# Low parts of the weights: an accumulating transfer onto a negated high part, in place of a VectorE subtraction

## The chip, the core and the metric

The kernel runs on one core of one Trainium2 chip. The metric is the device time of one execution in microseconds, the median of several runs. The kernel before takes 2429.83 us (three runs, 2429.18 to 2433.76). The engines are named as the profile names them: PE (TensorE, with PEld for its weight loads), DVE (VectorE), ACT (ScalarE), POOL (GpSimd), SP (SyncE, which here only issues transfers).

## What is computed

Two blocks of a language model in float32, one behind the other, on 512 tokens of width 1024. The first block has two layers: a hybrid mixer (gated linear attention beside stick-breaking attention) and a convolution mixer, each followed by a SwiGLU of width 2816. The second block has differential attention and a short convolution, each followed by a squared-ReLU MLP of width 4096. Cut to what matters here, everything the change touches is a product of activations with a weight:

```python
def swiglu(h, wg, wu, wd):
    return (jax.nn.silu(h @ wg) * (h @ wu)) @ wd

def sq_relu_mlp(x, w_up, w_down):
    return jnp.square(jax.nn.relu(x @ w_up)) @ w_down
```

## The kernel before

PE multiplies in a format (float32r) that keeps fewer bits than float32. The kernel therefore splits each operand into a high part (the value rounded to float32r) and a low part (the value minus the high part), and forms each product as three matmuls, in `mm3`: high weight by high input, high weight by low input, low weight by high input (L297, L298, L299).

A weight arrives by SP's queue in a buffer `wraw` of 128 x 2048 elements (1 MB; three such buffers), from `load_w` (L286) or `load_blocks` (L477, L480). `w_parts` turns half a buffer at a time, called a part here (128 x 1024 elements, 512 KB), into a tile `wh` and a tile `wl`, of which there are four each:

```python
act.activation(v(wh), src, AF.Copy)
dve.tensor_sub(v(wl), src, v(b(wh)))
```

ACT's line reads as L102 in the profile, since all ACT instructions go through one wrapper; DVE's is L273. There are 488 parts in the program.

Two kinds of stage use them. In most stages (`group` and its relatives: projections, and `out_proj`) a part meets all 512 tokens: eight blocks of 128 x 128, three matmuls each. In the up projections, `group_s` multiplies 2 x 2 blocks of weights and inputs in seven products instead of eight. It loads two `wraw` buffers, with the blocks b11, b12 in the first and b21, b22 in the second, and needs seven parts: b11, b22 and b21 as they are loaded, and four that DVE forms in place in `wraw`. A product is 8 blocks x 3 matmuls of 256 columns. There are 34 calls, in 14 runs of calls between two `out_proj`: 3, 4 and 3 in each SwiGLU (L856), and 1, 2, 2 and 2 in each MLP (L1398); the first group of each of the four layers is a plain one. The order of the code in a call is:

```python
o11 = parts(b11)
dve.tensor_sub(b11, b12, b11)           # L524
product(g, parts(b11), sums(0), True)
o22 = parts(b22)
dve.tensor_sub(b12, b22, b12)           # L533
dve.tensor_sub(b22, b11, b22)           # L534
product(a, parts(b22), sums(1))
```

Then follow the product with `o22`, those of b12 and b21, `dve.tensor_add(b21, b21, b22)` (L547), and the product of the new b21. Since L524, L534 and L547 overwrite a block that has just been split, each must wait until everything that reads the old block is done. ACT also copies three of the products out of PSUM (p1, p5, u2), and applies the activation function and the split of the results, in `evac`.

A scheduler gives every engine one fixed order of instructions from the program text; each engine then takes its list in that order, waiting at whatever is not ready. POOL's list before holds 173 rows: small set-up work and elementwise sums such as L862 (`pool_e.tensor_add` in SwiGLU's `down_evac`) and L406, L1092 (sums of squares).

Of the kernel before, what the change touches and what calls it, by code (L numbers as in the profile page):

```python
# [12 lines left out]
AF = mybir.ActivationFunctionType  # L13
# [96 lines left out]
def body(ctx: ExitStack, tc: tile.TileContext, A, out, consts):  # L110
    nc = tc.nc
    real_act, dve, pool_e, pe, sync = nc.scalar, nc.vector, nc.gpsimd, nc.tensor, nc.sync

    act = Act(tc, real_act)
# [70 lines left out]
    b = lambda t: t.bitcast(F32)  # L185
# [81 lines left out]
    def w_parts(src, n):  # L267
        n_p[0] += 1
        wh = wpool.tile([P, 1024], F32R, tag="wh", name=f"wh{n_p[0]}", bufs=4)
        wl = wpool.tile([P, 1024], F32R, tag="wl", name=f"wl{n_p[0]}", bufs=4)  # L270
        v = (lambda t: t[:, :n]) if len(src.shape) == 2 else (lambda t: t[:, :n].rearrange("p (k c) -> p k c", k=src.shape[1]))
        act.activation(v(wh), src, AF.Copy)
        dve.tensor_sub(v(wl), src, v(b(wh)))  # L273
        return wh, wl

    def load_w(parts, k0, nk):

        n_w[0] += 1
        i = n_w[0]
        cols = sum(c1 - c0 for _, c0, c1 in parts)  # L280
        n = nk * cols
        raw = wpool.tile([P, 2048], F32, tag="wraw", name=f"wraw{i}", bufs=3)
        rv = raw[:, :n].rearrange("p (k c) -> p k c", k=nk)
        o = 0
        for ap, c0, c1 in parts:
            sync.dma_start(rv[:, :, o : o + c1 - c0], ap[k0 * P : (k0 + nk) * P, c0:c1].rearrange("(k p) c -> p k c", p=P))  # L286
            o += c1 - c0
        assert nk % 2 == 0
        hi, lo = [], []
        for h in range(2):  # L290
            wh, wl = w_parts(raw[:, h * n // 2 : (h + 1) * n // 2], n // 2)
            for t, ks in ((wh, hi), (wl, lo)):
                ks += [t[:, k * cols : (k + 1) * cols] for k in range(nk // 2)]
        return hi, lo
# [189 lines left out]
    def group_plain(w0, w1, evac, at):  # L484


        ws = []
        for rv in load_blocks(w0, w1):
            for h in range(2):
                wh, wl = w_parts(rv[:, 2 * h : 2 * h + 2, :].rearrange("p k c -> p (k c)"), 1024)  # L490
                ws += [(wh[:, k * T : (k + 1) * T], wl[:, k * T : (k + 1) * T]) for k in range(2)]
        for th, tr in enumerate((T0, T1)):
            pss = [bank(), bank()]
            for k in range(8):
                for n in range(2):
                    for p in range(2):
                        wh, wl = (t[:, n * 256 + p * P : n * 256 + (p + 1) * P] for t in ws[k])
                        mm3(pss[n][:, p * 256 : (p + 1) * 256], wh, wl, xh[k][:, tr], xl[k][:, tr], k == 0 and p == 0, k == 7)
                if (th, k) in at:
                    at[th, k]()  # L500
            for n in (1, 0):
                evac(n, th, pss[n], False)

    def group_s(w0, w1, evac):
# [13 lines left out]
        xs = lambda k0, tr: lambda k: (xh[k0 + k][:, tr], xl[k0 + k][:, tr])  # L518
        sums = lambda n: lambda k: (so[0][:, k, n, :], so[1][:, k, n, :])
        parts = lambda t: w_parts(t, 1024)  # L520

        a, d, g = bank(), bank("at"), bank("at")
# [981 lines left out]
```

## Time and profile before

| | |
|---|---|
| Median of 3 runs | 2429.83 us |
| The profiled execution's own time | 2430.2 us |
| Its span, first to last instruction | 2428.4 us |
| PE, PEld busy | 2374.3, 2056.2 us |
| DVE busy, instructions | 1576.9 us, 2105 |
| ACT busy, instructions | 1185.1 us, 2005 |
| POOL busy, instructions | 218.8 us, 193 |
| SP's transfers | 204.72 MB, 26.0% of 16 engines' span |
| Mean granted TensorE clock | 0.988 |

Shares are of the span. PE's busy time counts overlapping matmuls and says little of its rate; how far apart matmuls start, in the rows in order of time, says more. A DMA share is the busy share of the core's 16 DMA engines. The granted clock is a share of 2.4 GHz, so 0.50 is 1.2 GHz.

### The profile page before, as it was taken

How to read it: one execution, taken by the hardware profiler on the slowest of the kernel's cores; microseconds unless marked ns; L12 is line 12 of the kernel's file. 1: busy time of each engine (PE TensorE's matmuls, PEld its weight loads, DVE VectorE, ACT ScalarE, POOL GpSimd, SP SyncE). 2: the span in 40 equal slices, each digit the busy share in tenths (PEclk: the TensorE clock that was granted, in tenths of full speed). 3: DMA queues.
4: the chain of work that ended last, by engine and by line, in shares of the span. 5: the costliest groups of instructions: out<-in, count | busy, mean ns of one | idle time of the engine just before them, and what ended most of it. 6: DMA issues, size and time to landing. Idle time of an engine off the chain costs nothing. (4 is left out here: it accounts for less than half of the span.)

```text
span 2428.4 us, 34281 instructions
## 1 busy us (share of the span) xinstructions
PE 2374.3 (98%) x14106; PEld 2056.2 (85%) x14106; DVE 1576.9 (65%) x2105; ACT 1185.1 (49%) x2005; POOL 218.8 (9%) x193
## 2 busy tenths in 40 slices
PE   8999999999999899999999999899999999899998
PEld 6667798989887799898987778898998888888998
DVE  4333685868799978585755775754577644854664
ACT  4663553434664655252444555653554224653553
POOL 0000000111002210202000003100003102100001
PEclk9999999999999899999999999999999999999999
DMA  5112223232312023232332112222332232223331
GB/s 166 36 52 70 70 84 108 88 122 70 122 53 69 18 70 122 87 105 91 111 108 66 53 53 70 87 71 95 130 101 74 87 104 78 79 71 104 122 99 41
DMA packets 148109, 206.91 MB, mean 85 GB/s; under 512 B 5822, under 2 KB 88305, under 8 KB 147953
## 3 DMA queue, kind: packets, MB, share of 16 engines
q1 hardware_dynamic: 147921, 204.72, 26.0%
q8 instruction: 110, 1.80, 0.3%
q14 instruction: 46, 0.38, 0.0%
q10 hardware_dynamic: 32, 0.01, 0.0%
HBM read 202.61 MB, written 2.10 MB: 84 GB/s over the span
## 5 line engine op out<-in xcount | busy, mean ns | idle before, releaser
L297 PE MATMUL ps<-rs,wh 128*128 128x256 f32 (+1 forms) x3216 | 1084.9, 338 | 9.4 <-ACT rs L102 4.1
L299 PE MATMUL ps<-rs,wl 128*128 128x256 f32 (+1 forms) x3216 | 1081.3, 337 | 10.3 <-DVE wl L273 10.3
L298 PE MATMUL ps<-rs,wh 128*128 128x256 f32 (+1 forms) x3216 | 1080.8, 336 | 0.0
L273 DVE TENSOR_TENSOR wl<-wraw,wh 128x1024 fp32r<-128x1024 f32 (+1 forms) x488 | 597.2, 1232 | 482.0 <-ACT wh L102 480.4
L102 ACT ACTIVATE wh<-wraw 128x1024 fp32r<-128x1024 f32 (+1 forms) x488 | 508.3, 1047 | 673.3 <-PE ps L298 546.1
L297 PEld LDWEIGHTS ps<-rs,wh 128*128 128x128 f32 x3216 | 611.1, 190 | 78.3 <-ACT rs L102 4.8
L299 PEld LDWEIGHTS ps<-rs,wl 128*128 128x128 f32 x3216 | 611.1, 190 | 77.7 <-DVE wl L273 12.1
L298 PEld LDWEIGHTS ps<-rs,wh 128*128 128x128 f32 x3216 | 610.8, 190 | 67.7 <-issue 2.9
L102 ACT ACTIVATE fs<-fs 128x512 f32<-128x512 f32 (+2 forms) x365 | 205.2, 571 | 93.6 <-DVE fs L1154 20.2
L299 PE MATMUL ps<-ph_so,wl 128*128 128x256 f32 x816 | 233.9, 287 | 4.1 <-DVE wl L273 3.9
L297 PE MATMUL ps<-ph_so,wh 128*128 128x256 f32 x816 | 232.6, 285 | 3.7 <-ACT wh L102 3.5
L298 PE MATMUL ps<-ph_so,wh 128*128 128x256 f32 x816 | 231.7, 284 | 0.0
L102 ACT ACTIVATE fs<-ps 128x512 f32<-128x512 f32 (+1 forms) x202 | 112.6, 562 | 138.0 <-PE ps L299 106.1
L299 PEld LDWEIGHTS ps<-ph_so,wl 128*128 128x128 f32 x816 | 157.5, 193 | 7.5 <-DVE wl L273 7.5
L297 PEld LDWEIGHTS ps<-ph_so,wh 128*128 128x128 f32 x816 | 157.5, 193 | 4.9 <-ACT wh L102 4.4
L298 PEld LDWEIGHTS ps<-ph_so,wh 128*128 128x128 f32 x816 | 157.5, 193 | 0.0
L102 ACT ACTIVATE rs<-fs 128x512 fp32r<-128x512 f32 (+1 forms) x153 | 91.9, 607 | 84.9 <-DVE fs L846 45.3
L429 DVE TENSOR_TENSOR rs<-fs,rs 128x512 fp32r<-128x512 f32 (+1 forms) x132 | 86.6, 663 | 18.3 <-ACT rs L102 17.9
L862 POOL TENSOR_TENSOR fs<-fs,fs 128x512 f32<-128x512 f32 x32 | 52.3, 1634 | 474.3 <-DVE fs L860 474.3
L102 ACT ACTIVATE rs<-fs,vec 128x256 fp32r<-128x256 f32 (+1 forms) x104 | 58.4, 585 | 62.0 <-POOL fs L1122 19.0
L406 POOL TENSOR_TENSOR fs<-fs,fs 128x512 f32<-128x512 f32 x28 | 46.3, 1653 | 385.7 <-ACT fs L102 373.7
L955 PE MATMUL ps<-rs,rs 128*128 128x256 f32 (+20 forms) x339 | 71.3, 364 | 1.1 <-DVE rs L1045 0.6
(303 smaller groups left out, 2160.9 us busy)
## 6 DMA issues: line engine op xcount, KB each, us to landing
wraw<-in_mlp_w_up_dram SPq DMA_DIRECT2D x32, 1024.0 KB
wraw<-in_mlp_w_down_dram SPq DMA_DIRECT2D x32, 1024.0 KB
wraw<-in_ffn_w_up_dram SPq DMA_DIRECT2D x44, 512.0 KB
wraw<-in_ffn_w_gate_dram SPq DMA_DIRECT2D x44, 512.0 KB
wraw<-in_ffn_w_down_dram SPq DMA_DIRECT2D x20, 1024.0 KB
wraw<-in_cv_w_pw_dram SPq DMA_DIRECT2D x16, 512.0 KB
wraw<-in_attn_w_qkv_dram SPq DMA_DIRECT2D x16, 512.0 KB
wraw<-in_conv_w_in_dram SPq DMA_DIRECT2D x16, 512.0 KB
```

Source lines behind the costliest of these rows:

```text
L102: r = self.engine.activation(out, in_, func, **kw)
L273: dve.tensor_sub(v(wl), src, v(b(wh)))
L297: pe.matmul(ps, wh, h, start=start, stop=False, skip_group_check=True)
L298: pe.matmul(ps, wh, l, start=False, stop=False, skip_group_check=True)
L299: pe.matmul(ps, wl, h, start=False, stop=stop, skip_group_check=True)
L406: r = eng.tensor_add(acc, acc, s)
L429: dve.tensor_sub(l, src, b(h))
L862: pool_e.tensor_add(res[o], res[o], s)
L955: pe.matmul(pc[:, y - t0 : t1 - t0], d, x[:, y - s : t1 - s], start=i == 0, stop=i == len(todo) - 1, skip_group_check=True)
```

## The change

`w_parts` alone changes. ACT writes the high part twice: once into `wh`, and once, times -1, into `wl`. The low part then comes about in `wl` by a transfer that GpSimd issues: it reads the raw weight and adds it to what `wl` holds, so that `wl` becomes weight minus high part. DVE's subtraction is gone. The lines below it in the file move down by one (L524 becomes L525 and so on).

```diff
--- before.py
+++ after.py
@@ -270,7 +270,8 @@
         wl = wpool.tile([P, 1024], F32R, tag="wl", name=f"wl{n_p[0]}", bufs=4)
         v = (lambda t: t[:, :n]) if len(src.shape) == 2 else (lambda t: t[:, :n].rearrange("p (k c) -> p k c", k=src.shape[1]))
         act.activation(v(wh), src, AF.Copy)
-        dve.tensor_sub(v(wl), src, v(b(wh)))
+        act.activation(v(wl), src, AF.Copy, scale=-1.0)
+        nc.gpsimd.dma_start(out=v(wl), in_=src, accum_op=mybir.AluOpType.add)
         return wh, wl
 
     def load_w(parts, k0, nk):
```

Every part therefore loses one DVE instruction, gains one ACT instruction and one transfer of 512 KB within SBUF. 488 transfers join POOL's list, which grows from 173 rows to 661; DVE's shrinks from 2104 to 1616 and ACT's grows from 1808 to 2321.

On ACT, in one call of `group_s` in the first SwiGLU (the call with part numbers 82 to 88 and the buffers wraw34, wraw35; `fs` are scratch tiles, `ps` PSUM banks, `rs` split activations; what a row waits for stands in brackets), the order before was:

```order
L102 ACTIVATE wh82_3734<-wraw34_3725 128x1024 [waits DMAHW7_49,PE_49]
L102 ACTIVATE fs17_98<-fs17_98 128x512 [waits DVE_49]
L102 ACTIVATE wh83_3764<-wraw34_3725 128x1024 [waits DVE_49,PE_49,Activation_49]
L102 ACTIVATE wh84_3793<-wraw35_3728 128x1024 [waits DMAHW2_49,PE_49,Activation_49]
L102 ACTIVATE fs23_104<-fs23_104 128x512 [waits DVE_49]
L102 ACTIVATE rs11_76<-fs17_98 128x2x256 [waits DVE_49]
L102 ACTIVATE rs11_76<-fs23_104 128x2x256 [waits DVE_49]
L102 ACTIVATE fs26_107<-ps139_3731 128x512 [waits PE_49]
L102 ACTIVATE wh85_3799<-wraw35_3728 128x1024 [waits DVE_49,Activation_49]
L102 ACTIVATE wh86_3855<-wraw34_3725 128x1024 [waits Activation_49]
L102 ACTIVATE wh87_3886<-wraw35_3728 128x1024 [waits DMAHW1_49,PE_49,Activation_49]
```

and is now, up to the fourth part:

```order
L102 ACTIVATE wh82_3815<-wraw34_3806 128x1024 [waits DMAHW7_49,Activation_49]
L102 ACTIVATE fs23_104<-fs23_104 128x512 [waits DVE_49]
L102 ACTIVATE wl82_3816<-wraw34_3806 128x1024 [waits DMASW5_49]
L102 ACTIVATE rs11_76<-fs17_98 128x2x256 [waits DVE_49]
L102 ACTIVATE wh83_3846<-wraw34_3806 128x1024 [waits DVE_49,PE_49,Activation_49]
L102 ACTIVATE rs11_76<-fs23_104 128x2x256 [waits DVE_49]
L102 ACTIVATE wl83_3847<-wraw34_3806 128x1024 [waits DMASW6_49,PE_49]
L102 ACTIVATE fs26_107<-ps139_3812 128x512 [waits PE_49]
L102 ACTIVATE wh84_3876<-wraw35_3809 128x1024 [waits DMAHW2_49,Activation_49]
L102 ACTIVATE wl84_3877<-wraw35_3809 128x1024 [waits DMASW7_49]
L102 ACTIVATE wh85_3883<-wraw35_3809 128x1024 [waits DVE_49]
```

Each `wh` is followed by a `wl`, with work on the results of the call before in between. `wh83`, the split of the new b11, still stands behind DVE's subtraction, and so does `wh85`.

On DVE, at the same place, from the first part's low part to the second's, before:

```order
L273 TENSOR_TENSOR wl82_3735<-wraw34_3725,wh82_3734 128x1024 [waits DMAHW7_49,Activation_49]
L524 TENSOR_TENSOR wraw34_3725<-wraw34_3725 128x4x256 [waits DMAHW0_49,DVE_49]
L542 TENSOR_TENSOR fs23_104<-ps136_3506,fs23_104 128x512 [waits PE_49]
L533 TENSOR_TENSOR wraw34_3725<-wraw35_3728,wraw34_3725 128x4x256 [waits DMAHW2_49,DVE_49]
L843 TENSOR_TENSOR fs23_104<-fs23_104,fs11_92 128x512 [waits DVE_49]
L545 TENSOR_TENSOR fs16_97<-ps137_3507,fs16_97 128x512 [waits PE_49]
L273 TENSOR_TENSOR wl83_3765<-wraw34_3725,wh83_3764 128x1024 [waits Activation_49]
```

and now, from the first subtraction in place to the last:

```order
L525 TENSOR_TENSOR wraw34_3806<-wraw34_3806 128x4x256 [waits DMAHW0_49,DMAHW7_49,DMASW6_49,DMASW1_49]
L847 TENSOR_TENSOR fs23_104<-ps136_3580,fs23_104 128x512 [waits PE_49]
L534 TENSOR_TENSOR wraw34_3806<-wraw35_3809,wraw34_3806 128x4x256 [waits DMAHW2_49,DVE_49]
L430 TENSOR_TENSOR rs13_78<-fs23_104,rs11_76 128x2x256 [waits Activation_49]
L535 TENSOR_TENSOR wraw35_3809<-wraw34_3806,wraw35_3809 128x4x256 [waits DMASW3_49,DMASW6_49,DVE_49,Activation_49]
L540 TENSOR_TENSOR fs24_105<-ps141_3814,fs24_105 128x512 [waits Activation_49]
L548 TENSOR_TENSOR wraw35_3809<-wraw35_3809 128x4x256 [waits DMAHW1_49,DMASW6_49,DVE_49]
```

The low parts (L273) are gone from the list, and the in-place operations on b11, b22 and b21 (L525, L535, L548) now wait for a transfer of GpSimd's queue (DMASW): that of part 82, 84 and 87, which read the old block.

On POOL, at the end of `out_proj` in the first SwiGLU, where L863 (L862 before) stood alone, now:

```order
L274 DMA wl102_4469<-wraw41_4466 128x1024 [waits DMAHW2_49,DMASW1_49,Activation_49]
L863 TENSOR_TENSOR fs3_84<-fs3_84,fs13_94 128x512 [waits DVE_49]
L274 DMA wl103_4474<-wraw41_4466 128x1024 [waits DMASW2_49,Activation_49]
L274 DMA wl104_4544<-wraw42_4534 128x4x256 [waits DMAHW3_49,DMASW3_49,Activation_49]
L863 TENSOR_TENSOR fs4_85<-fs4_85,fs9_90 128x512 [waits DVE_49]
L863 TENSOR_TENSOR fs5_86<-fs5_86,fs19_100 128x512 [waits DVE_49]
L274 DMA wl105_4575<-wraw42_4534 128x4x256 [waits DMASW4_49,Activation_49]
```

The transfers stand between POOL's sums in one list.

## Rows read from the trace of the kernel before

**Rows 1.** Page, part 1: busy time, share of the span, instructions of each engine.

```profile
PE 2374.3 (98%) x14106; PEld 2056.2 (85%) x14106; DVE 1576.9 (65%) x2105; ACT 1185.1 (49%) x2005; POOL 218.8 (9%) x193
```

**Rows 2.** Page, part 4: the chain that ended last, by engine.

```profile
PE 34%; DVE 4%; ACT 1%; issue 0%; POOL 0%; DVEq 0%; POOLq 0%
```

**Rows 3.** Waits of PE: line, releaser, total us, times, longest.

```profile
PE ps L299 <- DVE wl L273: 14.2, 11, 2.7
```

**Rows 4.** Page, part 5: groups by line; busy us, mean ns, idle before.

```profile
L273 DVE TENSOR_TENSOR wl<-wraw,wh 128x1024 fp32r<-128x1024 f32 (+1 forms) x488 | 597.2, 1232 | 482.0 <-ACT wh L102 480.4
L102 ACT ACTIVATE wh<-wraw 128x1024 fp32r<-128x1024 f32 (+1 forms) x488 | 508.3, 1047 | 673.3 <-PE ps L298 546.1
L862 POOL TENSOR_TENSOR fs<-fs,fs 128x512 f32<-128x512 f32 x32 | 52.3, 1634 | 474.3 <-DVE fs L860 474.3
```

**Rows 5.** ACT in order of time, 446 to 470 us: start, us, instruction, idle before.

```profile
446.67 0.64 ACT L102 ACTIVATE fs<-fs 128x512 f32<-128x512 f32 x1 [0.58 <-DVE fs L843]
449.15 1.06 ACT L102 ACTIVATE wh<-wraw 128x1024 fp32r<-128x1024 f32 x1 [1.84 <-DVE wraw L524]
...
453.74 0.64 ACT L102 ACTIVATE rs<-fs 128x512 fp32r<-128x512 f32 x1 [1.37 <-DVE fs L846]
...
456.61 0.58 ACT L102 ACTIVATE fs<-ps 128x512 f32<-128x512 f32 x1
...
462.58 0.60 ACT L102 ACTIVATE fs<-ps 128x512 f32<-128x512 f32 x1 [1.70 <-PE ps L299]
...
469.39 1.06 ACT L102 ACTIVATE wh<-wraw 128x1024 fp32r<-128x1024 f32 x1 [1.84 <-DVE wraw L524]
```

**Rows 6.** DVE in order of time, 445 to 470 us: start, us, instruction.

```profile
445.23 0.68 DVE L539 TENSOR_TENSOR fs<-ps,fs 128x512 f32<-128x512 f32 x1
...
446.56 1.22 DVE L273 TENSOR_TENSOR wl<-wraw,wh 128x1024 fp32r<-128x1024 f32 x1
447.81 1.23 DVE L524 TENSOR_TENSOR wraw<-wraw 128x1024 f32<-128x1024 f32 x1
...
468.05 1.22 DVE L524 TENSOR_TENSOR wraw<-wraw 128x1024 f32<-128x1024 f32 x1
```

**Rows 7.** PE in order of time, a 256-column stretch and a 512-column one.

```profile
447.33 0.28 PE L299 MATMUL ps<-rs,wl 128*128 128x256 f32 x1
447.45 0.28 PE L297 MATMUL ps<-rs,wh 128*128 128x256 f32 x1
...
18.71 0.40 PE L374 MATMUL ps<-wl,rs 128*128 128x512 f32 x1
18.95 0.40 PE L375 MATMUL ps<-wh,rs 128*128 128x512 f32 x1
```

**Rows 8.** Windows: length, busy us (x) by engine, PEclk, DMA share, GB/s.

```profile
core 0: us, PE busy (x) PEld busy (x) DVE busy (x) ACT busy (x) POOL busy (x), PEclk, DMA share, GB/s
447.80:468.00 20.20, 20.16 (x170) 19.96 (x169) 18.36 (x20) 11.30 (x14) 0.00 (x0) 1.00 0.35 108
439.50:444.00 4.50, 4.50 (x40) 4.50 (x40) 2.96 (x3) 2.97 (x4) 0.00 (x0) 1.00 0.60 191
820.00:840.00 20.00, 10.53 (x33) 8.04 (x34) 18.92 (x49) 11.02 (x29) 1.32 (x1) 0.62 0.04 12
1531.00:1552.00 21.00, 16.84 (x106) 15.83 (x107) 19.53 (x19) 14.19 (x23) 7.91 (x4) 0.84 0.12 41
```

**Rows 9.** Page, part 3: the queue that carries the weights: packets, MB, share.

```profile
q1 hardware_dynamic: 147921, 204.72, 26.0%
```

**Rows 10.** SP's issue of the first load, and PE's first matmul on it.

```profile
0.74 0.38 SPq L202 DMA_DIRECT2D ident<-consts_dram  x1
...
2.82 0.28 PE L255 MATMUL ps<-ident,ph_stage 16*128 16x16 f32 x1 [2.82 <-DMA ident<-consts_dram]
```


## The prediction

> **What bounds the kernel now.** I read the page's busy times first, then the chain, then what PE waits for. PE is busy for 98% of the span [rows 1], and the chain that ended last runs through PE for most of its named part [rows 2]. PE waits for a low part on 11 occasions, 14.2 us in all [rows 3]. So the work that the change takes away from DVE, 488 subtractions of 1232 ns, 597.2 us [rows 4], lies beside PE's; at most those 14.2 us and a little of the time at the ends of stages are to be won. What may be lost is larger, and the question is whether the new way of making a low part still keeps ahead of PE.
>
> How far ahead it must be is read from the rows in order of time. In a call of group_s, matmuls of 256 columns start 0.12 us apart (447.33, 447.45), so a product of 24 takes 24 x 0.118 = 2.83 us, and a new part is due every 2.83 us. The window shows the 0.118: 20.20 us for 170 matmuls, 7 x 24 = 168 of them [rows 7, 8]. In the other stages matmuls of 512 columns start 0.24 us apart [rows 7], and a part lasts 5.7 us. Two starts of L524 in calls that follow each other are 468.05 - 447.81 = 20.24 us apart: that is the period of a call, and PE is busy for 20.16 of 20.20 us in it [rows 6, 8].
>
> **Removed.** 597.2 us of DVE, beside PE: at most about 14 us on the path [rows 3, 4]. I take 0, since the wait that stood there comes back as a longer one.
>
> **Added on ACT.** 488 more writes of the kind that takes 1047 ns [rows 4], 511 us; ACT goes from 1185 to 1696 us of 2428, busy but no bound by sum.
>
> **Added on the DMA engines.** No row shows a transfer within SBUF or one that adds. The nearest rows are the weight loads: 191 GB/s at a share of 0.60, so 318 GB/s at full share [rows 8]. A part of 524,288 bytes takes 1.65 us at that rate if an adding transfer moves like a load; 3.3 us if reading both operands halves the rate; 6.6 us at a quarter. I take 3.3, because the destination has to be read as well as the source, and keep 1.65 and 6.6 as ends. In total 488 x 3.3 = 1610 us, plus 26.0% of 2428 = 631 us for the loads [rows 9]: 2241 us, below the span.
>
> The Trainium skill, in Collectives: The Full Stack, section The bandwidth ceiling, says the same of reductions in the DMA path: 32 against 62 GB/s, because the add needs two source reads. By it the term is the 3.3 us; no run here shows it yet.
>
> **The time to landing, L.** The first load's issue ends at 0.74 + 0.38 = 1.12 us, and PE starts on it at 2.82 [rows 10]: 1.7 us, of which 64 KB take 0.2, so 1.5 us are fixed. L is 1.5 + 1.65 = 3.2 us at the least and 1.5 + 6.6/0.83 = 9.5 at the most; I take 1.5 + 3.3/0.83 = 5.5, where 0.83 is what a call's loads leave free (0.35 of 20.2 us [rows 8] is 7 us, 17% of the 40 us that I find below). GpSimd's own time to issue a transfer is in no row; it is one reason to keep the upper end.
>
> The Trainium skill, in DMA: Bandwidth & Descriptors, section Anatomy of one DMA, fits GpSimd's transfers by 2.0 us plus bytes at 436 GB/s. By that estimate L is 3.2 us, and the sum would be that of the first rival.
>
> **One call of group_s.** Three operations in place on DVE (the new b11, b22, b21) now wait for a landed transfer, and behind each stands an ACT write, with everything else in ACT's list behind that. I walk round a call by durations of [rows 5, 6]: ACT write 1.06, DVE operation 1.23, ACT copy out of PSUM 0.58, activation or split 0.63, DVE sum 0.68.
> - From the issue of b11's transfer: L, L525 1.23, then on ACT wh 1.06, split 0.63, wl 1.06, copy of p1 0.58, b22's wh and wl 2.12. Together L + 6.7, and b22's transfer is issued.
> - From there: L, L535 1.23, wh 1.06, copy of p5 0.58, wl 1.06. Together L + 3.9, and the transfer of the new b22 is issued.
> - From there: L, then two products 5.66 and a sum 0.68 that stand ahead of L548 on DVE (b21's transfer, third in its queue, lands at about the same time, L + 6.6); L548 1.23; wh, activation and wl 2.74; the next call's wh, activation and wl 2.74. Together L + 13.0, and the next call's b11 is issued.
>
> Round the call: 3L + 23.6 = 40.1 us, against 20.24 now: 19.9 us more. Of the 34 calls, 20 follow another call and pay in full: 20 x 19.9 = 398 us. The first call of each of the 14 runs is prepared in part beneath the end of out_proj; four tiles of wl let that be two or three parts, so I charge half: 14 x 9.9 = 139 us.
>
> **The other parts**, 488 - 34 x 7 = 250, cost 0: the DMA engines need 3.3 + 1.65 us for one and for its load, PE takes 5.7, and four tiles allow 3 x 5.7 = 17 us of lead against 2 x 1.06 + 5.5. If that cover goes (a transfer of 6.6 us, 8.3 with its load), each costs 2.6 us, 650 in all.
>
> **Ends of stages.** Where PE already waits for a low part [rows 3] the subtraction of 1.23 us becomes 1.06 + 5.5: 11 x 5.3 = 58 us. POOL's sums, 1.6 us each [rows 4], and the transfers now wait for each other in one list. I cost that at 0, since the lead of 17 us hides it outside group_s; without it each of the 32 L863 delays a part by its 1.6 us, 52 us in all.
>
> **The clock.** In the span's worst gap, PE busy for 10.53 of 20 us, the granted clock was 0.62; at 16.84 of 21 it was 0.84 [rows 8]. In a call of 40 us PE would be busy for half. At 1.2 GHz the two products on the path take 5.66 us more, 34 x 5.66 = 192 us; I take half, 96, as the clock is low for part of the time.
>
> **Sum.** 2430 + 398 + 139 + 58 + 96 = 3121 us, made against the profiled execution (2430.2 us; the median is 2429.83, so no correction). I predict 3120 us. The measurement tells changes of about 0.2% (5 us) from none.
>
> **Rivals.**
> 1. *The transfers are cheap.* L = 3.2 and 1.65 us each. Round the call 3 x 3.2 + 23.6 = 33.2, 13 more: 20 x 13 + 14 x 6.5 = 351; ends 11 x 3.0 = 33; clock 0. 2815 us. For it: the engines are idle for two thirds of the time. Against it: it lets the second read cost nothing. Chance 0.17.
> 2. *The transfers become the bound*, by DMA engines at a quarter of a load's rate or by GpSimd's issue taking as long. 488 x 6.6 + 631 = 3850 us, with gaps some 3950. For it: nothing in the trace shows such a transfer's price. Against it: nothing shows one so slow. Chance 0.23.
> 3. *Faster.* DVE's freed time reaches PE's waits: the 14.2 us of [rows 3] go, 2416 us. It decides at the point where a second write and a landing take no longer than the subtraction: 1.06 + L below 1.23. The least fixed time, 1.5 us, is above that already. Chance 0.02.
> 4. *No effect.* The scheduler's lead hides all of it in group_s too. That needs a round of at most 20.24 us, which is less than its 23.6 without any L. Chance 0.01: 2430 us.
>
> **Numbers.** The forecast keeps 0.57. It is slower by over 0.2% in three cases, 0.57 + 0.17 + 0.23 = 0.97; faster 0.02; within 0.2% 0.01. The range reaches below the first rival (2815), as the part of a round that is hidden may be larger than I charge, and up to the second's: 2700 to 3950. It leaves out some 0.15: still slower transfers, and the two cases without a loss.
>
> **What would show it.** In the profile after: DVE's 488 subtractions gone, ACT's writes at about 976 and 1020 us, a GpSimd queue with 488 transfers and about 256 MB. Starts of L525 in calls that follow each other should be 36 to 45 us apart, with ACT idle before wh until DVE's L525, L535 and L548, and DVE idle until a transfer. Out_proj and the projections should stay near their old pace. I am wrong in the main step if the period of a call is below 30 us; wrong in the price of a transfer if the projections are stretched too, or if the transfers' share of the engines is far from 1610 us.

## The result, and the profile after

The changed kernel takes 3129.91 us (median of 4 runs, 3123.56 to 3132.5), 1.287 times the kernel before, 95% interval 1.2849 to 1.289. The forecast was 3120 us. The loss is 700 us.

The page of the profile after, line by line: busy times, the DMA queues, the chain that ended last, two groups of instructions, and the transfers with their size and median time to landing:

```profile
PE 2607.1 (84%) x14106; PEld 2223.7 (71%) x14106; DVE 1018.3 (33%) x1617; ACT 1610.7 (52%) x2493; POOL 710.0 (23%) x681
...
q0 software_dynamic: 161664, 252.80, 46.9%
q1 hardware_dynamic: 147921, 204.72, 20.2%
...
PE 12%; DMA 8%; issue 5%; ACT 4%; DVE 2%; POOL 1%; POOLq 0%; DVEq 0%; ACTq 0%
...
L274 POOL DMA_DIRECT2D wl<-wraw x488 | 523.7, 1074 | 2097.8 <-ACT wl L102 1885.5
...
L102 ACT ACTIVATE wl<-wraw 128x1024 fp32r<-128x1024 f32 (+1 forms) x488 | 504.8, 1034 | 15.3 <-PE ps L375 15.3
...
wl<-wraw POOLq DMA_DIRECT2D x476, 512.0 KB, 5.2
```

DVE is down to 1018.3 us from 1576.9 [rows 1], and it helped nothing: PE's share fell from 98% to 84%. ACT has its 488 second writes, 504.8 us (2493 instructions against 2005 [rows 1]). A queue that was not there before carries 252.80 MB at 46.9% of 16 engines, beside the loads' 20.2%; the loads themselves moved the same 204.72 MB as in [rows 9]. From the start of its issue on GpSimd a transfer takes 5.2 us to land. The chain could be followed back only to 2145 us, so its shares, 32% in all, speak of the last third of the span; the transfer has 8%.

Who waited for whom (engine, line, releaser: us in total, times, longest):

```profile
engine line waited for: us in total, times, longest us
PEld ps L300 <- DMA wl<-wraw: 408.2, 152, 6.4
...
DVE wraw L535 <- DMA wl<-wraw: 240.8, 33, 10.2
...
ACT wh L102 <- DVE wraw L535: 201.4, 32, 7.1
DVE wraw L525 <- DMA wl<-wraw: 196.7, 33, 37.6
...
ACT wh L102 <- DVE wraw L525: 159.5, 25, 11.4
...
ACT wh L102 <- DVE wraw L548: 70.2, 32, 3.5
...
DVE wraw L548 <- DMA wl<-wraw: 32.4, 20, 3.3
```

PE's weight loads wait 408 us for a landed low part, where before they waited 19.6 us for DVE's low part (PE's matmuls then: 14.2 us [rows 3]). The lines of DVE and ACT in pairs are the mechanism: DVE's L535 waits for a transfer, 240.8 us, and ACT's next split waits for L535, 201.4; the same for L525, 196.7 and 159.5. L548 waits for a transfer only 32.4 us in all, because L540 ahead of it on DVE has waited already; what releases it is read from one call below.

One call of group_s in order of time, the counterpart of [rows 5, 6]. ACT (start, us, instruction, idle before and what ended it):

```profile
543.25 1.06 ACT L102 ACTIVATE wh<-wraw 128x1024 fp32r<-128x1024 f32 x1 [5.78 <-DVE wraw L525]
...
546.16 1.04 ACT L102 ACTIVATE wh<-wraw 128x1024 fp32r<-128x1024 f32 x1
547.11 1.04 ACT L102 ACTIVATE wl<-wraw 128x1024 fp32r<-128x1024 f32 x1
555.27 1.06 ACT L102 ACTIVATE wh<-wraw 128x1024 fp32r<-128x1024 f32 x1 [7.12 <-DVE wraw L535]
...
556.71 1.05 ACT L102 ACTIVATE wl<-wraw 128x1024 fp32r<-128x1024 f32 x1
...
568.24 0.60 ACT L102 ACTIVATE fs<-ps 128x512 f32<-128x512 f32 x1 [6.70 <-PE ps L300]
571.13 1.06 ACT L102 ACTIVATE wh<-wraw 128x1024 fp32r<-128x1024 f32 x1 [2.29 <-DVE wraw L548]
```

DVE in the same call:

```profile
541.91 1.23 DVE L525 TENSOR_TENSOR wraw<-wraw 128x1024 f32<-128x1024 f32 x1 [3.72 <-DMA wl<-wraw]
...
554.01 1.23 DVE L535 TENSOR_TENSOR wraw<-wraw,wraw 128x1024 f32<-128x1024 f32 x1 [8.45 <-DMA wl<-wraw]
568.87 0.69 DVE L540 TENSOR_TENSOR fs<-ps,fs 128x512 f32<-128x512 f32 x1 [13.64 <-ACT fs L102]
569.81 1.22 DVE L548 TENSOR_TENSOR wraw<-wraw 128x1024 f32<-128x1024 f32 x1 [0.25 <-DMA wl<-wraw]
...
582.36 1.23 DVE L525 TENSOR_TENSOR wraw<-wraw 128x1024 f32<-128x1024 f32 x1 [3.24 <-DMA wl<-wraw]
```

POOL, the issue of the transfers of b22, of the new b22, of b21 and of the next call's b11:

```profile
548.44 1.28 POOL L274 DMA_DIRECT2D wl<-wraw  x1 [1.09 <-ACT wl L102]
558.05 1.28 POOL L274 DMA_DIRECT2D wl<-wraw  x1 [8.33 <-ACT wl L102]
...
561.84 1.28 POOL L274 DMA_DIRECT2D wl<-wraw  x1 [0.61 <-ACT wl L102]
...
576.96 1.30 POOL L274 DMA_DIRECT2D wl<-wraw  x1 [1.52 <-DVE fs L546]
```

ACT writes b22's negated high part from 547.11 on, for 1.04 us. GpSimd issues the transfer at 548.44. DVE's L535, which overwrites b22, starts at 554.01, after 8.45 us of waiting; ACT's next write starts when L535 has ended, at 555.27, after 7.12 us. Then ACT waits 6.70 us for the product that needs the new b22 (568.24), and L540 and L548 follow. L548 has one more wait: it starts at 569.81, 0.25 us after L540 has ended, when b21's transfer, issued at 561.84, has landed. By the issue and the landing of each transfer in the trace, L548 starts within 0.3 us of b21's landing in 29 of the 34 calls; so b21's is the third landing of the round, more often than the new b22's. From one L525 (541.91) to the next (582.36) it takes 40.45 us, against 20.24 before [rows 6].

Windows of the profile after: two calls in the first SwiGLU, one in the second, and the entry to an out_proj:

```profile
core 0: us, PE busy (x) PEld busy (x) DVE busy (x) ACT busy (x) POOL busy (x), PEclk, DMA share, GB/s
541.90:582.40 40.50, 28.07 (x164) 26.56 (x164) 10.89 (x14) 17.45 (x21) 8.97 (x7) 0.75 0.73 141
582.40:621.60 39.20, 26.33 (x168) 24.89 (x168) 10.81 (x13) 17.45 (x21) 8.96 (x7) 0.80 0.75 145
1113.80:1153.30 39.50, 25.50 (x169) 24.18 (x168) 11.65 (x15) 17.86 (x22) 8.95 (x7) 0.86 0.69 126
660.00:680.00 20.00, 15.48 (x66) 12.34 (x66) 1.39 (x2) 6.43 (x7) 2.57 (x3) 0.91 0.94 243
```

In a call PE is busy for 25 to 28 of 40 us at a clock of 0.75 to 0.86; before it was 20.16 of 20.20 at 1.00 [rows 8].

### The profile page after: what moved, and what is told of

Its sections match the earlier page's. It is cut to its first block, busy times and chain, and to the rows that moved or that the text cites. A ratio compares the mean times of both kernels' runs of the same rounds, so it can differ in the third digit from the quotient of the medians.

```text
span 3121.4 us, 35667 instructions
## 1 busy us (share of the span) xinstructions
PE 2607.1 (84%) x14106; PEld 2223.7 (71%) x14106; DVE 1018.3 (33%) x1617; ACT 1610.7 (52%) x2493; POOL 710.0 (23%) x681
## 3 DMA queue, kind: packets, MB, share of 16 engines
q0 software_dynamic: 161664, 252.80, 46.9%
q1 hardware_dynamic: 147921, 204.72, 20.2%
## 5 line engine op out<-in xcount | busy, mean ns | idle before, releaser
L298 PE MATMUL ps<-rs,wh 128*128 128x256 f32 (+1 forms) x3216 | 1124.8, 350 | 72.3 <-ACT wh L102 41.8
L299 PE MATMUL ps<-rs,wh 128*128 128x256 f32 (+1 forms) x3216 | 1111.3, 346 | 0.0
L274 POOL DMA_DIRECT2D wl<-wraw x488 | 523.7, 1074 | 2097.8 <-ACT wl L102 1885.5
L298 PEld LDWEIGHTS ps<-rs,wh 128*128 128x128 f32 x3216 | 645.2, 201 | 156.5 <-ACT wh L102 51.9
L299 PEld LDWEIGHTS ps<-rs,wh 128*128 128x128 f32 x3216 | 644.6, 200 | 67.3 <-issue 2.1
L102 ACT ACTIVATE wl<-wraw 128x1024 fp32r<-128x1024 f32 (+1 forms) x488 | 504.8, 1034 | 15.3 <-PE ps L375 15.3
L300 PE MATMUL ps<-ph_so,wl 128*128 128x256 f32 x816 | 282.6, 346 | 199.4 <-DMA wl<-wraw 199.3
L300 PEld LDWEIGHTS ps<-ph_so,wl 128*128 128x128 f32 x816 | 200.5, 246 | 214.6 <-DMA wl<-wraw 214.6
L298 PE MATMUL ps<-ph_so,wh 128*128 128x256 f32 x816 | 279.0, 342 | 45.1 <-ACT wh L102 41.6
L299 PE MATMUL ps<-ph_so,wh 128*128 128x256 f32 x816 | 270.6, 332 | 0.0
L298 PEld LDWEIGHTS ps<-ph_so,wh 128*128 128x128 f32 x816 | 199.1, 244 | 59.6 <-ACT wh L102 50.1
L299 PEld LDWEIGHTS ps<-ph_so,wh 128*128 128x128 f32 x816 | 198.3, 243 | 0.0
L540 DVE TENSOR_TENSOR fs<-ps,fs 128x512 f32<-128x512 f32 x34 | 23.5, 692 | 407.6 <-ACT fs L102 407.6
L535 DVE TENSOR_TENSOR wraw<-wraw,wraw 128x1024 f32<-128x1024 f32 x34 | 43.2, 1270 | 248.1 <-DMA wl<-wraw 240.8
L525 DVE TENSOR_TENSOR wraw<-wraw 128x1024 f32<-128x1024 f32 x34 | 41.7, 1225 | 197.7 <-DMA wl<-wraw 196.7
```

The lines of the kernel that those rows point to most:

```text
L102: r = self.engine.activation(out, in_, func, **kw)
L274: nc.gpsimd.dma_start(out=v(wl), in_=src, accum_op=mybir.AluOpType.add)
L298: pe.matmul(ps, wh, h, start=start, stop=False, skip_group_check=True)
L299: pe.matmul(ps, wh, l, start=False, stop=False, skip_group_check=True)
L300: pe.matmul(ps, wl, h, start=False, stop=stop, skip_group_check=True)
L540: dve.tensor_add(u2, g, u2)
```

## The experiments

The theory tested is that of the prediction: three operations in place per call of group_s wait for a landed transfer, and ACT's list stands behind each. Its rivals: every part costs something wherever it stands (bandwidth, GpSimd's issue); ACT's second write is the price; the clock is. Each kernel was timed beside the kernel before, whose median then lay between 2427.02 and 2428.13 us; ratios and losses go by that. A round is the time from one start of L524 (or its counterpart) to the next call's; there are 20 such intervals within runs of calls, 22.4 us each on average before and 40.5 in the changed kernel.

**Old low parts in group_s, transfers everywhere else.** group_s passes a flag, and `w_parts` then makes the low part the old way:

```diff
-    def w_parts(src, n):
+    def w_parts(src, n, s_call=False):
...
+        if s_call:
+            dve.tensor_sub(v(wl), src, v(b(wh)))
+            return wh, wl
...
-        parts = lambda t: w_parts(t, 1024)
+        parts = lambda t: w_parts(t, 1024, True)
```

> Edit: group_s makes its low parts on VectorE as before; the 250 parts of all other stages keep the accumulating transfer. Theory (the loss is the chain inside group_s, where three in-place operations wait for a landed transfer): nearly all of the 700 us goes, 2430 plus at most 60 for the ends of stages, 2440 to 2490 us, and L524 starts again 20 us apart. Rival (transfers or ACT's second writes cost by the part, wherever they are): 250 of 488 parts keep 250/488 of 700 us, about 2790 us.

Measured: 2459.29 us, 1.013 of the kernel before (1.0113 to 1.0147). The page's busy times and the new queue:

```profile
PE 2377.0 (97%) x14106; PEld 2050.7 (84%) x14106; DVE 1292.1 (53%) x1855; ACT 1395.3 (57%) x2255; POOL 418.5 (17%) x443
...
q0 software_dynamic: 36000, 128.01, 27.3%
```

Half of the bytes are still moved by transfers, and 32 us are lost instead of 700. The price is not one by the part. The 20 intervals are 22.4 us on average, as before the change.

**The opposite: transfers in group_s alone** (the same edit with `if not s_call`).

> Edit: the opposite of the run before, accumulating transfers in group_s alone (238 parts). Theory: 3130 less what the other stages cost (10 to 60), 3070 to 3120 us. Rival (cost by the part): 238/488 of 700 us, about 2770 us. If the two add up, the losses of both runs sum to 700 us.

Measured: 3033.24 us, 1.2491 (1.2472 to 1.2509), 606 us more than before and 37 below the expected range. So 238 parts make 606 of the 700 us, and 250 parts 32; 606 + 32 leave some 62 us that arise only together. The time between the last call of a run and the first of the next, which holds out_proj, shows where part of that lies: 60.8 us on average before, 61.8 in the first experiment, 78.9 in this one and 84.6 with all transfers (ten such stretches, from L524 to L524). The window of the entry to an out_proj here, which stands for the window 660 to 680 us above:

```profile
641.00:661.00 20.00, 20.00 (x95) 16.54 (x94) 7.04 (x8) 3.70 (x4) 2.68 (x3) 1.00 0.61 211
```

PE is busy throughout here, and for 15.48 of 20 us with all transfers, where loads and transfers together hold the DMA engines for 0.94 of the time instead of 0.61. That this crowding alone makes the difference was not isolated.

**ACT's second write without any transfer:**

```diff
-        nc.gpsimd.dma_start(out=v(wl), in_=src, accum_op=mybir.AluOpType.add)
+        dve.tensor_add(v(wl), src, v(b(wl)))
```

> Edit: ACT still writes the negated high part into wl, but VectorE adds the weight to it instead of a transfer. No transfer is left; ACT has all its 488 second writes. Theory: the second write costs little, since ACT in a call is busy for 11.3 + 7 x 1.04 = 18.6 of 20.2 us; a call becomes 20 to 23 us, 2430 to 2530 us. Rival (ACT's second write is the price): close to 3130 us.

Measured: 2567.36 us, 1.0572 (1.0552 to 1.0592); the expectation's upper end was missed by 37 us. The window of one call, from L525 to L525:

```profile
350.50:376.14 25.64, 24.50 (x203) 24.04 (x202) 21.16 (x25) 17.99 (x22) 0.00 (x0) 1.00 0.31 102
```

This interval, 20.24 us in the call of [rows 6], is 25.64 us long with ACT busy for only 18.0, so ACT is not full. (PE is busy through most of it because it holds 203 matmuls, 35 more than a call has.) The 20 intervals grew from 22.4 to 27.3 us on average, 4.9 each. Five of the seven second writes stand on the path of a round as the prediction walks it (those of b11', b22, b22', b21' and the next b11), and 5 x 1.04 = 5.2 us is close to that; which writes the path really holds was not isolated. So the second write with DVE's sum behind it costs 140 us without any transfer. In the changed kernel DVE has no such sum, so the 140 are not exactly a part of the 700.

**A transfer that copies instead of adding:**

```diff
-        nc.gpsimd.dma_start(out=v(wl), in_=src, accum_op=mybir.AluOpType.add)
+        nc.gpsimd.dma_start(out=v(wl), in_=src)
```

> Edit: the transfer copies the weight into wl without adding (so the low part is the whole weight; the write, the waits and the order stay). It measures what the second read costs. Theory: a copy moves at a load's rate, a part in 1.65 instead of about 2.9 us, so L falls from 5.2 to about 3.9; a round of three L is 4 us shorter, 3130 - 34 x 4 = about 2990 us, and the queue's share falls from 46.9% to about 27%. Rival (the reading of the destination costs nothing, it is all issue and latency): about 3130 us, share unchanged.

Measured, one run: 2832.57 us. The page's line on the queue, and that on the landing:

```profile
q0 software_dynamic: 161664, 252.80, 29.5%
...
wl<-wraw POOLq DMA_DIRECT2D x476, 512.0 KB, 3.2
```

The page's group of the issues on GpSimd, whose counterpart in the changed kernel is shown above:

```profile
L274 POOL DMA_DIRECT2D wl<-wraw x488 | 313.1, 642 | 2014.5 <-ACT wl L102 1746.6
```

So adding costs 5.2 - 3.2 = 2.0 us of landing: the engines take 252.80 MB at 46.9% of 3121 us = 173 GB/s, 3.0 us a part, against 303 GB/s (29.5% of 2831 us), 1.7 us, and the issue takes 1.07 instead of 0.64 us on average. A round falls from 40.5 to 34.0 us on average, 6.5, of which three landings are 6.0; the expected 4 us a round were too small because the landing fell by 2.0 and not by 1.3 us. The time fell by 297 us, where 140 were expected, and most of it outside those rounds: of the 291 us between the two profiled spans, 129 lie in the 20 intervals, 108 in the ten stretches around out_proj and 53 between the layers and at both ends. The theory's direction holds, its place in part. This kernel is also the first rival of the prediction made real: L = 3.2 us there gave 33.2 us a round and 2815 us.

**Early splits: the three landings overlap.**

```diff
         o11 = parts(b11)
+        o21 = parts(b21)
+        o22 = parts(b22)
+        product(a, o11, xs(0, T0), True)
         dve.tensor_sub(b11, b12, b11)
-        product(a, o11, xs(0, T0), True)
+        product(d, o21, xs(4, T0), True)
...
-        o22 = parts(b22)
...
-        product(a, parts(b22), sums(1))
+        n22 = parts(b22)
+        product(g, o22, sums(2))
+        product(a, n22, sums(1))
...
-        product(g, o22, sums(2))
...
-        product(d, parts(b21), xs(4, T0), True)
```

> Edit: in group_s the blocks that are split as they are loaded (b11, b21, b22) are split first, one after the other, before any operation in place, and the products of b21 and of b22 come earlier so that wl tiles free up in turn. Parts, transfers and ACT writes stay the same in number. Theory (three landings in series in one round): the three landings overlap, a round becomes about ACT's own 14 x 1.04 + 8 = 23 us and a few more, 25 to 28 us, and the kernel 2430 + 34 x 6 + 90 = about 2720, 2620 to 2800 us. Rival (a transfer has its price wherever it stands, by bandwidth or by GpSimd's issue): within 60 us of 3130.

Measured: 2866.17 us, 1.1799 (1.1778 to 1.1819). The same parts, transfers and writes in another order win 264 us, where 330 to 510 were expected; a round takes 31.9 us on average, not 25 to 28. Two calls:

```profile
510.97:542.70 31.73, 25.27 (x170) 24.30 (x170) 11.78 (x15) 19.81 (x24) 8.98 (x7) 0.87 0.88 160
542.70:574.15 31.45, 24.64 (x168) 23.42 (x168) 9.20 (x11) 16.85 (x21) 8.96 (x7) 0.89 0.96 182
```

The DMA engines are busy for 0.88 and 0.96 of the call: with the landings overlapped they look like the bound. Seven transfers of 3.0 us and 2.1 MB of loads at 325 GB/s, 6.5 us, are 27.5 us of a round. That was tested by the early splits with the copy of the fourth experiment:

```diff
-        nc.gpsimd.dma_start(out=v(wl), in_=src, accum_op=mybir.AluOpType.add)
+        nc.gpsimd.dma_start(out=v(wl), in_=src)
```

> Edit: the early splits, with transfers that copy without adding (the low part is the whole weight). Theory (with early splits a round of 31.5 us is bound by the DMA engines, busy for 0.88 to 0.96 of it): a copy takes 1.73 instead of 3.0 us of the engines, 7 x 1.73 + 6.5 = 18.6 us a round, so the bound becomes ACT and a round 25 to 28 us, the kernel 2600 to 2700 us. Rival (wl and wh tiles or the order on PE bind the round): it stays near 31 us, 2800 us or more.

Measured, one run: 2628.88 us. Two calls, at the same place:

```profile
475.20:500.20 25.00, 22.13 (x175) 21.16 (x176) 11.74 (x15) 16.76 (x21) 5.18 (x7) 1.00 0.77 214
500.20:523.40 23.20, 20.54 (x160) 19.30 (x160) 9.13 (x12) 16.92 (x21) 5.18 (x7) 1.00 0.89 245
```

These two calls take 25.0 and 23.2 us, at a clock of 1.00; the 20 intervals are 27.4 us on average. So without the second read a round is 4.5 us shorter again, and tiles or PE's order do not hold it at 31. A copy also lands sooner (3.2 us), so engine time and time to landing are not told apart. Some 200 us above the kernel before are left.

**Filler on PE.** 48, 24 and 24 matmuls ahead of three products:

```diff
+        junk = bank("at")
+        def filler(n):
+            for _ in range(n):
+                pe.matmul(junk[:, :256], xh[0][:, :P], xh[0][:, T1], start=True, stop=True, skip_group_check=True)
...
+        filler(48)
         product(g, n11, sums(0), True)
```

> Edit: the changed kernel, with 96 matmuls of 256 columns per call of group_s into a bank that nobody reads, placed where PE waits (48 ahead of the second product, 24 ahead of the third, 24 ahead of the seventh), 11 us of a round of 40 at full clock. Theory (part of the loss is the clock: 0.75 to 0.86 in calls of group_s): the clock stays near 1.0, the two products on the path take 2.8 instead of about 5 us, a round becomes 2 to 4 us shorter, 3000 to 3060 us although more is computed. Rival (the clock is beside the path): 3130 us or more.

Measured: 3092.78 us, 1.2732 (1.2693 to 1.2772), 37 us below the changed kernel, so above the range that the theory gave. Two calls:

```profile
539.40:578.50 39.10, 34.33 (x272) 34.13 (x271) 10.81 (x14) 17.35 (x21) 8.98 (x7) 0.91 0.74 143
578.50:618.20 39.70, 34.28 (x264) 34.08 (x263) 10.86 (x14) 17.35 (x21) 8.97 (x7) 0.91 0.75 147
```

The product behind the new b22's landing, in the changed kernel and here, and the wait of L557, which is L548 of the changed kernel (packets are counted in the window they start in, so a DMA share in so short a one can pass 1):

```profile
563.10:568.20 5.10, 5.06 (x22) 4.77 (x22) 0.00 (x0) 0.00 (x0) 0.02 (x1) 0.50 1.23 192
560.00:564.90 4.90, 4.89 (x24) 4.89 (x25) 0.00 (x0) 0.03 (x1) 0.46 (x1) 0.55 1.24 193
...
DVE wraw L557 <- DMA wl<-wraw: 326.8, 25, 14.5
```

The mean clock in a call rises from 0.75 and 0.80 to 0.91, and a round is 39.1 us on average instead of 40.5. But the theory is not borne out by this. The filler itself ran at full clock (24 matmuls took 3.04 us in this call); behind its end PE still waited for the landing (4.77 us in this call), and the product on the path then ran at 0.55, against 0.50 in the changed kernel. Over all 34 calls the time from that landing to ACT's copy of the product is 4.5 us on average here and 3.8 there. L557 meanwhile starts with b21's landing, and DVE's order changed too (the sum of L540 now stands behind it). What the 37 us come from stays open; they do not show a price of the clock.

**The negated high part by DVE.**

```diff
-        act.activation(v(wl), src, AF.Copy, scale=-1.0)
+        dve.tensor_scalar(v(wl), src, -1.0, None, ALU.mult)
```

> Edit: VectorE instead of ACT writes the negated high part into wl (one operation on the weight, times -1); the accumulating transfer stays. Theory (five of a call's second writes lie on its path, as the run without transfers showed with 25.6 instead of 20.2 us): they leave ACT's list and run on VectorE beside ACT's write of wh; a round becomes 35 to 37 instead of 40.4 us, the kernel 2950 to 3030 us. Rival (the Trainium skill, SBUF - State Buffer, on VectorE's copies that hold GpSimd up while it writes descriptors): GpSimd's issue of a transfer grows beyond 1.28 us and L beyond 5.2, and the time stays at 3080 us or more.

Measured: 2984.94 us, 1.2283 (1.224 to 1.2325); a round takes 36.4 us on average. The theory's numbers are met, and the rival's time is not. GpSimd's issue of a transfer takes longer here, as the rival says, but the rows give another reason. The page's group, all issues by length, and three issues in order of time:

```profile
L274 POOL DMA_DIRECT2D wl<-wraw x488 | 552.6, 1296 | 1889.6 <-DVE wl L273 1094.1
...
L274 POOL DMA_DIRECT2D wl<-wraw x488: 841/1279/2396, 12.6 to 2944.5; - x163
...
344.78 4.09 POOL L274 DMA_DIRECT2D wl<-wraw  x3 [7.67 <-PE ps L300]
```

DVE's write, 0.69 us in the median, and its longest one beside two sums on GpSimd:

```profile
L273 DVE TENSOR_SCALAR wl<-wraw x488: 417/687/2937, 11.6 to 2942.2; 128x1024 fp32r<-128x1024 f32 x158, 128x512 fp32r<-128x512 f32 x3, 128x544 fp32r<-128x544 f32 x2
...
1410.56 2.80 POOL L863 TENSOR_TENSOR fs<-fs,fs 128x512 f32<-128x512 f32 x2
1410.98 2.94 DVE L273 TENSOR_SCALAR wl<-wraw 128x1024 fp32r<-128x1024 f32 x1
```

The issue grew from 1.07 to 1.30 us on average, and landing takes 6.6 us instead of 5.2. The Trainium skill, SBUF — State Buffer, section SBUF: two separate sides, says that GpSimd cannot write the descriptors of its transfers while VectorE runs a copy that uses both of its ports; the trace does not show that as the cause. None of the 34 issues over 2.2 us has a DVE instruction beside it. Each follows other issues that have not ended, as DVE now makes three parts within 1.9 us where ACT took 1.9 us for each, and its transfer lands after some 9 us. Whether DVE's writes also delay an issue by some tenths of a microsecond is not separated here. What the longer issues and landings cost the kernel was not isolated.

**Transfers where DVE is the bound.**

```diff
+        if not by_transfer[0]:
+            dve.tensor_sub(v(wl), src, v(b(wh)))
+            return wh, wl
...
+    by_transfer[0] = True
     for c in range(4):
...
+    by_transfer[0] = False
```

> Edit: transfers only for the weights of the convolution mixer's first projection, where VectorE is busy for 60 of 60 us before (700 to 760 us); everything else as before the change. Theory: in the run with the old way in group_s this stretch was 304.0 instead of 309.5 us long, so 5 us are won: 0.998 of before, 2421 to 2425 us. Rival (the second write and the issue cost as much as VectorE gains): 2427 us or more.

Measured: 2425.03 us, 0.9985 (0.9976 to 0.9994), in 11 runs against 15. The page's busy times:

```profile
PE 2368.5 (98%) x14106; PEld 2053.8 (85%) x14106; DVE 1558.4 (64%) x2089; ACT 1199.6 (50%) x2021; POOL 229.6 (9%) x209
```

Sixteen parts by transfer in the convolution mixer win 3 us, 0.15%, the upper end of the expectation: the stretch from the last L524 before it to the first behind it (590.37 to 894.48) is 304.1 us long, against 309.5 before (593.49 to 902.99) and 304.0 in the first experiment. These are single executions, whose unchanged stretches also differ by up to 3 us. This is the only version faster than the kernel before, and by little.

## Why the prediction was right

- **What bounds.** Right: PE's lead over its low parts decided, and DVE's 597 us beside PE were worth 3 us, in one mixer.
- **The price of a transfer.** I took 3.3 us of the engines; it is 3.0. L was 5.5; it is 5.2. The reason given, the second read, holds: without it 1.7 and 3.2 us. By an estimate from the Trainium skill's rule in Collectives: The Full Stack, section The bandwidth ceiling (half the rate for two reads), it would be 3.4; measured 173 against 303 GB/s, 0.57. By an estimate from the Trainium skill's fit in DMA: Bandwidth & Descriptors, section Anatomy of one DMA, L would be 3.2 us; that is what a copy takes here, and an adding transfer takes 2.0 us more.
- **The round.** 3L + 23.6 = 40.1 us was forecast, 40.45 measured at one place and 40.5 on average over the 20 intervals (809 us in all). The three stretches of the walk come out too: from b11's issue to b22's 12.6 us on average (forecast 12.2), on to the new b22's 9.8 (9.4), on to the next b11's 18.1 (18.5). The third is right partly by luck. Two products behind the new b22's landing were forecast, 5.66 us at full clock. In the call shown one stands there, as the product with o22 had run while PE waited, and at a clock of 0.50 it took 5.1 us; and L548 mostly follows b21's landing, which the walk put at about the same time. Before, those 20 intervals are 448 us, 22.4 each and not 20.24, as the second call of some runs starts late; they grew by 361 us, where I had 398.
- **The first calls: this term was mis-sized.** I charged half a round's excess for the first call of a run, 139 us for 14. The ten stretches around out_proj grew by 238 us, 23.8 each, and the three long stretches between layers and the two ends by 94 us together. With transfers in group_s alone those ten grew by 18.1 us each, as much as a round there (18.2): nothing of the price of a call is hidden beneath out_proj. The rest comes only when out_proj's own parts go by transfer as well.
- **The other parts and the ends of stages.** 0 and 58 us forecast; 32 us measured for all of them together with the old group_s. In company of the new group_s some 62 us more.
- **The clock: 96 us that no run shows.** The clock did fall to 0.75 to 0.86 in calls, but I put its price on products that seldom decide when L548 starts, and the filler did not raise the clock of the product on the path. What the clock costs of the 700 us stays open.
- **The sum.** 3120 against 3130 us is closer than its terms, and that is luck: 37 us too much within runs of calls and 96 for the clock, which the measured stretches already hold, stand against 332 us outside the rounds where I had 139 + 58 = 197. The mechanism, three landings in series in a call, is what the runs show. No run gave the new blocks a buffer of their own, so the overwriting was not tested apart from the order of the work.
- **Rivals.** The cheap transfer fell by the copy's run, which shows what it would have been. The transfers as the bound fell for this order of work, at 0.73 of the engines in a call; with early splits they come near to it, 0.88 to 0.96. Faster and no effect fell by the result.

## What to carry to other kernels

Before an operation moves from an engine to a transfer, look for what overwrites the transfer's source: that writer waits for a landing where it waited for an instruction, and everything behind it in its list with it. Count landings in series in one period, since three landings of 5.2 us, with ACT's second writes, cost 18 us a call here, and 250 parts with four tiles of lead cost 32 us together. Where the transfer must stay, split what is there first and overwrite afterwards (264 us here), and expect the second read to count next (another 237 us, if the copy is the measure).

## What was not expected of the hardware

An adding transfer costs GpSimd more to issue than a copy of the same shape, 1.07 against 0.64 us on average. PE's granted clock fell to 0.75 in calls where PE still had work for 28 of 40 us, and filler work raised the mean to 0.91 but left the product behind the wait at 0.55. A write by DVE of 0.69 us in the median took up to 2.94 us in the kernel of the negated part by DVE: all 13 writes over 1.3 us ran beside a sum on GpSimd (the longest beside two of L863), while beside an issue alone none took over 1.1 us.
